# The decayed scores of a recurrence, one block size at a time: 64 strided query columns per size

## The chip, the cores and the metric

The kernel runs on one core of one Trainium2 chip. The metric is the device time of one execution in microseconds (us). A profile of one execution gives the busy time of each engine: TensorE (PE, with its weight loads as PEld), VectorE (DVE), ScalarE (ACT), GpSimd (POOL) and SyncE (SP, which issues the transfers).

## The reference, cut to what matters

One encoder layer over 16 meta tokens and 256 tokens, width 2048. Half of the mixing width is a recurrence with eight heads of width 128, whose keys decay by a forget gate per channel; the other half is a retention with four heads. A projection ahead of them, an output projection, two layer norms and a gated feed-forward block follow the usual way. What the change touches is the recurrence's scores:

```python
q = silu(q) * HG_HEAD_DIM ** -0.5
forget = lb + (1.0 - lb) * sigmoid(f_pre)
log_f, k = log(forget), 1.0 - forget
...
cum = cumsum(log_f)                     # over the tokens
decay = exp(where(causal, cum[t] - cum[s], -inf))      # per channel
scores = einsum('bhtk,bhsk,bhtsk->bhts', q, k, decay)
out = einsum('bhts,bhsv->bhtv', scores, v) + ...
```

So the score of query t and key s is the sum over 128 channels of q times k times the product of the forget gates from s + 1 to t. For t = s it is the plain product of q and k.

## The kernel before, in words

Weights come in blocks of 128 x 2048 fp32. ScalarE rounds a block to fp32r (`whi`, L75), VectorE takes the rest (`wlo`, L76), and each product of the projections is three matmuls (`whi` with the high part of the activations, `wlo` with it, `whi` with their low part). Three buffers hold each half, so a block's cast waits until TensorE has finished the block three before it. `project` (L317) uses one block for 128 output rows: 48 matmuls of 272 or 256 columns. `token_group` (L131) uses four blocks for a gate or the queries: 96 matmuls of 512 columns.

The recurrence and the retention are laid into this stream. `project` calls `tick` after every 12 matmuls, `token_group` after every 6; `steps` is a queue of pairs (ticks to wait, function), and a step issues its work when its ticks are over. The recurrence is done for a pair of heads at a time, `hgrn(pr, ...)`, four pairs: in pairs 0 and 2 a gate's `token_group` and then the retention's projections follow, in pairs 1 and 3 the retention's projections at once.

In `hgrn`, channels lie on partitions and tokens on the free axis: `Q` and `K` are 128 x 512 (two heads of 256 tokens; `K` has the meta tokens behind), `F` the forget gates. The scores `S` are 128 keys by 128 queries for each of four chunks. They are built by doubling: for block size b, a query in the second half of a block of 2b tokens meets the keys of its first half. `update(b)` then multiplies the queries of each second half by the decay of the first (`across(Q, ...)`), the keys of each first half by that of the second (`across(K, ...)`), and multiplies the block decays pairwise (`double`). Before, two sizes share one step: `E` holds three copied sets of 64 query columns per chunk, `scores` multiplies all of them with `K` in one product of 192 columns per chunk (L443, two PSUM banks of the name `sc`), and `merge` copies each set under a mask into `S` (L455). The diagonal is masked by the identity out of the first step's product (L488). `level32` (L517) and `level64` (L508) do the two largest sizes, `cross` (L528) the second 128 queries against the first 128 keys, `meta_scores` (L542) the meta tokens. `read_out` multiplies `S` with the values.

A scheduler sets the order on each engine from the order in which the code issues work; the engines run their own queues in order and wait for each other by semaphores.

Of the kernel before, what the change touches and what calls it, by code (L numbers as in the profile page):

```python
# [9 lines left out]
F32 = mybir.dt.float32  # L10
F32R = mybir.dt.float32r
I32 = mybir.dt.int32
# [26 lines left out]
def encoder_kernel(ctx: ExitStack, tc: tile.TileContext, x, meta, par, rows, w_in, w_out,  # L39
# [136 lines left out]
    make_identity(nc, ident)  # L176
    nhalf = cpool.tile([P, 8], F32, name="nhalf")
# [167 lines left out]
    with tc.tile_pool(name="att", bufs=1) as att:  # L345
        msk = att.tile([P, 7, 64], I32, name="msk")
# [35 lines left out]
        def hgrn(pr, qt, get_g):  # L382
# [29 lines left out]
            E = att.tile([P, 3, 4 * 64], F32, name="E")  # L412
# [24 lines left out]
            def scores():  # L437

                scs = []
                for o in (0, 2):  # L440
                    sc = pss.tile([P, 512], F32, name="sc")
                    for c in range(2):
                        nc.tensor.matmul(sc[:, c * 192:(c + 1) * 192], K[:, (o + c) * P:(o + c + 1) * P],  # L443
                                         E[:, :, (o + c) * 64:(o + c + 1) * 64], start=True, stop=True)
                    scs.append(sc[:, :384].rearrange("p (c m t) -> p c m t", c=2, m=3))
                return scs

            def targets(o, b):

                return [S[:, o:o + 2, :].rearrange("p c (n two b) -> p c n two b", two=2, b=b)[:, :, :, x, :]  # L450
                        for x in (1, 0)]

            def merge(scs, b, m, mask):
                for o, sc in zip((0, 2), scs):
                    nc.vector.copy_predicated(  # L455
                        out=targets(o, b)[0],
                        mask=msk[:, mask:mask + 1, :].broadcast_to([P, 2, 64]).rearrange("p c (n b) -> p c n b", b=b),
                        data=sc[:, :, m, :].rearrange("p c (n b) -> p c n b", b=b))

            def prepare(b):  # L460

                n = 2 * SEQ // (4 * b)
                nc.scalar.copy(E[:, 0, :].rearrange("p (n b) -> p n b", b=b), pairs(Q, b)[:, :, 1, :])
                across(Q, b, 2 * SEQ, True)
                far = pairs(Q, 2 * b)[:, :, 1, :]
                nc.scalar.copy(E[:, 1, :].rearrange("p (n b) -> p n b", b=2 * b), far)
                dv = state["d"][:, :2 * SEQ // b].rearrange("p (n four) -> p n four", four=4)
                nc.vector.tensor_tensor(out=E[:, 2, :].rearrange("p (n b) -> p n b", b=2 * b), in0=far,
                                        in1=dv[:, :, 1:2].broadcast_to([P, n, 2 * b]), op=ALU.mult)

            def first_queries():
                qv, fv = pairs(Q, 1), pairs(F, 1)
                state["d"] = F
                for x in range(2):
                    nc.scalar.copy(E[:, x, :], qv[:, :, x, 0])
                nc.vector.tensor_tensor(out=E[:, 2, :], in0=qv[:, :, 1, 0], in1=fv[:, :, 1, 0], op=ALU.mult)

            def levels_0_1():
                scs = scores()
                nc.vector.tensor_tensor(out=Q, in0=Q, in1=F[:, :2 * SEQ], op=ALU.mult)  # L480
                across(K, 1, W, False)
                across(Q, 1, 2 * SEQ, True)
                double(1)
                prepare(2)
                for o, sc in zip((0, 2), scs):
                    for x in range(2):
                        unit = ident.rearrange("p (n two) -> p n two", two=2)[:, :, x]
                        nc.vector.tensor_tensor(out=targets(o, 1)[1 - x][:, :, :, 0], in0=sc[:, :, x, :],  # L488
                                                in1=unit.unsqueeze(1).broadcast_to([P, 2, 64]), op=ALU.mult)
                merge(scs, 1, 2, 0)  # L490

            def levels(b, mask):
                scs = scores()
                across(K, b, W, False)
                double(b)
                across(Q, 2 * b, 2 * SEQ, True)
                across(K, 2 * b, W if 2 * b <= 8 else 2 * SEQ, False)
                double(2 * b)
                if b == 2:
                    prepare(8)  # L500
                merge(scs, b, 0, mask)
                merge(scs, 2 * b, 1, mask + 1)
                merge(scs, 2 * b, 2, mask + 2)

            def level64():
                sc = pss.tile([P, 512], F32, name="sc")
                for c in range(4):
                    nc.tensor.matmul(sc[:, c * 64:(c + 1) * 64], K[:, c * P:(c + 1) * P],  # L508
                                     Q[:, c * P + 64:(c + 1) * P], start=True, stop=True)
                update(64)  # L510
                nc.scalar.copy(S[:64, :, 64:], sc[:64, :256].rearrange("p (c t) -> p c t", c=4))
# [389 lines left out]
def _constants():  # L901
# [8 lines left out]
    for b in (2, 8):  # L910
        masks.append(level(b)[:, i // b % 2 == 1])
        for x in (1, 0):
            masks.append((level(2 * b) & (s // b % 2 == x))[:, i // (2 * b) % 2 == 1])
# [78 lines left out]
```

## Time and profile before

| | |
|---|---|
| median of 3 runs | 1293.54 us (1293.52 to 1295.84) |
| the profiled execution | 1293.27 us |
| its span, first to last instruction | 1291.5 us |
| busy: TensorE, VectorE, ScalarE, GpSimd | 98%, 58%, 42%, 1% of the span |
| mean granted TensorE clock | 0.997 of full speed |

The recurrence's steps lie between 62 and 432 us of the span. Times of rows are in us from the span's start. An fp32 product of the code is two matmul records in the trace.

### The profile page before, as it was taken

The page shows a single profiled execution, that of the slowest core. Times are in us where ns is not written, and L with a number is a line of the kernel's source. Part 1 is how long each engine was busy: PE and PEld are TensorE (multiplying, and loading weights), DVE is VectorE, ACT ScalarE, POOL GpSimd, SP SyncE. Part 2 cuts the span into 40 slices and gives each one's busy share as a digit, 9 for nine tenths or more (in the row PEclk, how much of TensorE's full clock was granted, in tenths as well). Part 3 has the DMA queues.
Part 4 walks back from the last instruction along what each step waited for, and adds up shares of the span by engine and source line. Part 5 has one row for each costly group of instructions (what it writes and reads, how often), then busy time and mean ns, then how long its engine had stood idle before and what let it go on. Part 6 is the DMA issues. An engine that isn't in the chain of part 4 may idle for free.

```text
span 1291.5 us, 17602 instructions
## 1 busy us (share of the span) xinstructions
PE 1266.2 (98%) x7516; PEld 1128.8 (87%) x7516; DVE 751.7 (58%) x872; ACT 547.1 (42%) x570; POOL 13.7 (1%) x27
## 2 busy tenths in 40 slices
PE   6999999999999999999999999999999999999996
PEld 4989999898999988878888888888888888888886
DVE  7765575565566585675555555444455555554565
ACT  7534334343343333574444444333344444444340
POOL 0000000000000000000000000000000000000000
PEclk9999999999999999999999999999999999999998
DMA  6644444444444377565555555455555555555551
GB/s 233 250 152 163 164 143 142 163 174 150 148 159 159 137 293 260 195 228 196 194 181 183 192 195 191 171 193 195 195 199 192 196 189 183 186 192 184 191 179 66
DMA packets 34958, 237.56 MB, mean 184 GB/s; under 512 B 4016, under 2 KB 4656, under 8 KB 6960
## 3 DMA queue, kind: packets, MB, share of 16 engines
q1 hardware_dynamic: 34880, 236.44, 52.1%
q8 instruction: 59, 0.97, 0.3%
q14 instruction: 19, 0.16, 0.0%
HBM read 234.33 MB, written 2.10 MB: 183 GB/s over the span
## 4 chain that ended last, share of the span: by engine, by line
PE 96%; DVE 1%; ACT 1%; DMA 0%; POOL 0%; issue 0%; SPq 0%; POOLq 0%; DVEq 0%
PE pp L131 34%; PE pp L841 23%; PE pp L317 22%; PE pp L846 12%; PE sc L443 1%; PE pp L123 1%; PE sc L623 1%; DMA xt<-in_x_dram 0%; ACT fl L225 0%; PE ms L555 0%; PE ms L552 0%; PE ms L375 0%; PE sc L542 0%; PE ms L636 0%; PE ms L635 0%; PE sc L508 0%
## 5 line engine op out<-in xcount | busy, mean ns | idle before, releaser
L76 DVE TENSOR_TENSOR wlo<-raw,whi 128x2048 fp32r<-128x2048 f32 (+1 forms) x211 | 479.0, 2271 | 391.9 <-ACT whi L75 390.2
L75 ACT CAST whi<-raw 128x2048 fp32r<-128x2048 f32 (+1 forms) x211 | 399.3, 1893 | 379.9 <-PE pp L131 202.7
L841 PE MATMUL pp<-h,whi 128*128 128x512 f32 x1280 | 305.4, 391 | 0.0
L841 PEld LDWEIGHTS pp<-h,whi 128*128 128x128 f32 x1280 | 235.3, 188 | 45.6
L317 PE MATMUL pp<-xhi,whi 128*128 128x272 f32 (+1 forms) x768 | 225.1, 293 | 0.0
L317 PE MATMUL pp<-xlo,whi 128*128 128x272 f32 (+1 forms) x768 | 219.9, 286 | 0.0
L317 PE MATMUL pp<-xhi,wlo 128*128 128x272 f32 (+1 forms) x768 | 219.1, 285 | 0.0
L131 PE MATMUL pp<-whi,t 128*128 128x512 f32 x648 | 199.8, 389 | 0.0
L846 PEld LDWEIGHTS pp<-h,wlo 128*128 128x128 f32 x1280 | 164.0, 191 | 6.2
L846 PE MATMUL pp<-h,wlo 128*128 128x256 f32 x1280 | 166.1, 283 | 0.0
L317 PEld LDWEIGHTS pp<-xhi,wlo 128*128 128x128 f32 x768 | 144.8, 189 | 0.4
L317 PEld LDWEIGHTS pp<-xhi,whi 128*128 128x128 f32 x768 | 144.7, 188 | 0.5
L317 PEld LDWEIGHTS pp<-xlo,whi 128*128 128x128 f32 x768 | 144.6, 188 | 0.0
L131 PEld LDWEIGHTS pp<-whi,t 128*128 128x128 f32 x648 | 121.6, 188 | 25.1
L131 PE MATMUL pp<-wlo,t 128*128 128x512 f32 x324 | 126.1, 389 | 0.0
L131 PEld LDWEIGHTS pp<-wlo,t 128*128 128x128 f32 x324 | 60.8, 188 | 12.6
L131 PE MATMUL pp<-whi,xhi 128*128 128x512 f32 x128 | 52.4, 412 | 1.8 <-ACT xhi L229 1.8
L131 PE MATMUL pp<-whi,xlo 128*128 128x512 f32 x128 | 51.2, 400 | 0.4 <-DVE xlo L230 0.4
L131 PE MATMUL pp<-wlo,xhi 128*128 128x512 f32 x128 | 51.5, 402 | 0.0
L131 PE MATMUL pp<-whi,mhi 128*128 128x512 f32 x120 | 46.9, 391 | 0.0
L131 PE MATMUL pp<-whi,mlo 128*128 128x512 f32 x120 | 46.7, 389 | 0.0
L131 PE MATMUL pp<-wlo,mhi 128*128 128x512 f32 x120 | 46.7, 389 | 0.0
(203 smaller groups left out, 963.8 us busy)
## 6 DMA issues: line engine op xcount, KB each, us to landing
raw<-in_w_gu_dram SPq DMA_DIRECT2D x88, 1024.0 KB, 4.9
raw<-in_w_in_dram SPq DMA_DIRECT2D x62, 1024.0 KB, 4.8
raw<-in_w_down_dram SPq DMA_DIRECT2D x44, 1024.0 KB, 4.9
raw<-in_w_out_dram SPq DMA_DIRECT2D x16, 1024.0 KB, 4.9
gb<-in_rows_dram SPq DMA_DIRECT2D x6, 1024.0 KB, 7.7
raw<-in_w_in_dram SPq DMA_DIRECT2D x4, 512.0 KB, 8.0
acc<-in_x_dram SPq DMA_DIRECT2D x2, 1024.0 KB, 6.0
out_dram<-acc SPq DMA_DIRECT2D x6, 256.0 KB, 2.4
```

The costliest lines, as they stand in the source:

```text
L75: nc.scalar.copy(hi[:, sl], raw[:, sl])
L76: nc.vector.tensor_tensor(out=lo[:, sl], in0=raw[:, sl], in1=hi[:, sl].bitcast(F32), op=ALU.subtract)
L123: nc.tensor.matmul(ph[:, :256], a, ws[k // 4][w][:, c:c + 256], start=(k == 0 and m == 0), stop=(k == 4 * n - 1 and m == 2))
L131: nc.tensor.matmul(ps[i], a, w[:, j * 512:(j + 1) * 512], start=(seen[i] == 0), stop=(left[i] == 0 and j == 3 and m == 2))
L317: nc.tensor.matmul(ps[:, :n], w[:, kc, :], a[:, kc, T - n:], start=(kc == 0 and j == 0), stop=(kc == KC - 1 and j == 2))
L443: nc.tensor.matmul(sc[:, c * 192:(c + 1) * 192], K[:, (o + c) * P:(o + c + 1) * P], E[:, :, (o + c) * 64:(o + c + 1) * 64], start=True, st ...
L623: nc.tensor.matmul(sc[:, c0:c0 + n], RK[:, k, k0:k0 + P], RQ[:, k, q0:q0 + n], start=(k == 0), stop=(k == 1))
L841: nc.tensor.matmul(ps, hi[:, kc, :], h[:, kc].rearrange("p m t -> p (m t)"), start=(kc == 0), stop=False)
L846: nc.tensor.matmul(ps[:, :SEQ], lo[:, kc, :], h[:, kc, 0, :], start=False, stop=(kc == KC - 1))
```

## The change

For each block size from 1 to 32 a step takes its 64 query columns per chunk straight out of `Q` with a stride, one product of 64 columns per chunk, and writes only one PSUM bank. The copies into `E` go. The diagonal comes from `own` = Q times K, multiplied with a column of ones (one column per chunk), and is spread by four activations over the identity. There are eight steps up to `level64` instead of six, and 29 ticks up to `meta_scores` instead of 25.

```diff
@@ -174,6 +174,8 @@
 
     ident = cpool.tile([P, P], F32, name="ident")
     make_identity(nc, ident)
+    ones = cpool.tile([P, 1], F32, name="ones")
+    nc.gpsimd.memset(ones, 1.0)
     nhalf = cpool.tile([P, 8], F32, name="nhalf")
     nc.gpsimd.memset(nhalf, -0.5)
 
@@ -343,7 +345,7 @@
     lnp_ctx.close()
 
     with tc.tile_pool(name="att", bufs=1) as att:
-        msk = att.tile([P, 7, 64], I32, name="msk")
+        msk = att.tile([P, 5, 64], I32, name="msk")
         nc.sync.dma_start(msk, masks)
         rp = att.tile([P, 2, T], F32, name="rp")
         nc.sync.dma_start(rp, rope)
@@ -409,7 +411,6 @@
 
 
 
-            E = att.tile([P, 3, 4 * 64], F32, name="E")
 
             def pairs(t, b, w=2 * SEQ):
                 return t[:, :w].rearrange("p (n two b) -> p n two b", two=2, b=b)
@@ -434,92 +435,47 @@
                 across(K, b, w, False)
                 double(b)
 
-            def scores():
-
-                scs = []
-                for o in (0, 2):
-                    sc = pss.tile([P, 512], F32, name="sc")
-                    for c in range(2):
-                        nc.tensor.matmul(sc[:, c * 192:(c + 1) * 192], K[:, (o + c) * P:(o + c + 1) * P],
-                                         E[:, :, (o + c) * 64:(o + c + 1) * 64], start=True, stop=True)
-                    scs.append(sc[:, :384].rearrange("p (c m t) -> p c m t", c=2, m=3))
-                return scs
-
-            def targets(o, b):
-
-                return [S[:, o:o + 2, :].rearrange("p c (n two b) -> p c n two b", two=2, b=b)[:, :, :, x, :]
-                        for x in (1, 0)]
-
-            def merge(scs, b, m, mask):
-                for o, sc in zip((0, 2), scs):
-                    nc.vector.copy_predicated(
-                        out=targets(o, b)[0],
-                        mask=msk[:, mask:mask + 1, :].broadcast_to([P, 2, 64]).rearrange("p c (n b) -> p c n b", b=b),
-                        data=sc[:, :, m, :].rearrange("p c (n b) -> p c n b", b=b))
-
-            def prepare(b):
-
-                n = 2 * SEQ // (4 * b)
-                nc.scalar.copy(E[:, 0, :].rearrange("p (n b) -> p n b", b=b), pairs(Q, b)[:, :, 1, :])
-                across(Q, b, 2 * SEQ, True)
-                far = pairs(Q, 2 * b)[:, :, 1, :]
-                nc.scalar.copy(E[:, 1, :].rearrange("p (n b) -> p n b", b=2 * b), far)
-                dv = state["d"][:, :2 * SEQ // b].rearrange("p (n four) -> p n four", four=4)
-                nc.vector.tensor_tensor(out=E[:, 2, :].rearrange("p (n b) -> p n b", b=2 * b), in0=far,
-                                        in1=dv[:, :, 1:2].broadcast_to([P, n, 2 * b]), op=ALU.mult)
-
-            def first_queries():
-                qv, fv = pairs(Q, 1), pairs(F, 1)
-                state["d"] = F
-                for x in range(2):
-                    nc.scalar.copy(E[:, x, :], qv[:, :, x, 0])
-                nc.vector.tensor_tensor(out=E[:, 2, :], in0=qv[:, :, 1, 0], in1=fv[:, :, 1, 0], op=ALU.mult)
-
-            def levels_0_1():
-                scs = scores()
-                nc.vector.tensor_tensor(out=Q, in0=Q, in1=F[:, :2 * SEQ], op=ALU.mult)
-                across(K, 1, W, False)
-                across(Q, 1, 2 * SEQ, True)
-                double(1)
-                prepare(2)
-                for o, sc in zip((0, 2), scs):
-                    for x in range(2):
-                        unit = ident.rearrange("p (n two) -> p n two", two=2)[:, :, x]
-                        nc.vector.tensor_tensor(out=targets(o, 1)[1 - x][:, :, :, 0], in0=sc[:, :, x, :],
-                                                in1=unit.unsqueeze(1).broadcast_to([P, 2, 64]), op=ALU.mult)
-                merge(scs, 1, 2, 0)
-
-            def levels(b, mask):
-                scs = scores()
-                across(K, b, W, False)
-                double(b)
-                across(Q, 2 * b, 2 * SEQ, True)
-                across(K, 2 * b, W if 2 * b <= 8 else 2 * SEQ, False)
-                double(2 * b)
-                if b == 2:
-                    prepare(8)
-                merge(scs, b, 0, mask)
-                merge(scs, 2 * b, 1, mask + 1)
-                merge(scs, 2 * b, 2, mask + 2)
-
-            def level64():
+            def odd_scores(b):
+
                 sc = pss.tile([P, 512], F32, name="sc")
                 for c in range(4):
                     nc.tensor.matmul(sc[:, c * 64:(c + 1) * 64], K[:, c * P:(c + 1) * P],
-                                     Q[:, c * P + 64:(c + 1) * P], start=True, stop=True)
-                update(64)
-                nc.scalar.copy(S[:64, :, 64:], sc[:64, :256].rearrange("p (c t) -> p c t", c=4))
+                                     pairs(Q, b)[:, c * 64 // b:(c + 1) * 64 // b, 1, :], start=True, stop=True)
+                return sc[:, :256].rearrange("p (c t) -> p c t", c=4)
+
+            def first():
+
+                own = att.tile([P, 2 * SEQ], F32, name="own", tag="sq")
+                nc.vector.tensor_tensor(out=own, in0=Q, in1=K[:, :2 * SEQ], op=ALU.mult)
+                dg = pss.tile([P, 512], F32, name="sc")
+                for c in range(4):
+                    nc.tensor.matmul(dg[:, c:c + 1], own[:, c * P:(c + 1) * P], ones, start=True, stop=True)
+                nc.vector.tensor_tensor(out=Q, in0=Q, in1=F[:, :2 * SEQ], op=ALU.mult)
+                state["d"] = F
+                od = att.tile([P, 4], F32, name="od")
+                nc.scalar.copy(od, dg[:, :4])
+                for c in range(4):
+                    nc.scalar.activation(S[:, c, :], ident, AF.Identity, scale=od[:, c:c + 1])
+
+            def level(b, mask):
+                sc = odd_scores(b)
+                update(b)
+                for o in (0, 2):
+                    nc.vector.copy_predicated(
+                        out=S[:, o:o + 2, :].rearrange("p c (n two b) -> p c n two b", two=2, b=b)[:, :, :, 1, :],
+                        mask=msk[:, mask:mask + 1, :].broadcast_to([P, 2, 64]).rearrange("p c (n b) -> p c n b", b=b),
+                        data=sc[:, o:o + 2, :].rearrange("p c (n b) -> p c n b", b=b))
 
             def level32():
-                sc = pss.tile([P, 512], F32, name="sc")
-                for c in range(4):
-                    for o in (0, 64):
-                        nc.tensor.matmul(sc[o:o + 32, c * 32:(c + 1) * 32], K[:, c * P + o:c * P + o + 32],
-                                         Q[:, c * P + o + 32:c * P + o + 64], start=True, stop=True)
+                sc = odd_scores(32)
                 update(32)
                 for o in (0, 64):
-                    nc.scalar.copy(S[o:o + 32, :, o + 32:o + 64],
-                                   sc[o:o + 32, :128].rearrange("p (c t) -> p c t", c=4))
+                    nc.scalar.copy(S[o:o + 32, :, o + 32:o + 64], sc[o:o + 32, :, o // 2:o // 2 + 32])
+
+            def level64():
+                sc = odd_scores(64)
+                update(64)
+                nc.scalar.copy(S[:64, :, 64:], sc[:64])
 
             def cross():
 
@@ -582,11 +538,10 @@
                     nc.vector.scalar_tensor_tensor(out=mlo[:, h, :], in0=ot[:, j * SEQ:(j + 1) * SEQ], scalar=g,
                                                    in1=mhi[:, h, :].bitcast(F32), op0=ALU.mult, op1=ALU.subtract)
 
-            steps.append((2, first_queries))
-            steps.append((2, levels_0_1))
-            steps.append((5, lambda: levels(2, 1)))
-            steps.append((5, lambda: levels(8, 4)))
-            steps.append((4, level32))
+            steps.append((4, first))
+            for n in range(5):
+                steps.append((3, lambda n=n: level(1 << n, n)))
+            steps.append((3, level32))
             steps.append((3, level64))
             steps.append((2, cross))
             steps.append((2, meta_scores))
...
-    masks = [level(1)[:, 1::2]]
-    for b in (2, 8):
-        masks.append(level(b)[:, i // b % 2 == 1])
-        for x in (1, 0):
-            masks.append((level(2 * b) & (s // b % 2 == x))[:, i // (2 * b) % 2 == 1])
+    masks = [level(b)[:, i // b % 2 == 1] for b in (1, 2, 4, 8, 16)]
```

On TensorE, the steps of the first pair between the value transposes (`ms<-ident,vt`) and `cross`. The projection matmuls between the rows are left out. Before:

```order
L443 MATMUL sc<-E,K 128x192 x4
...
L375 MATMUL ms<-ident,vt 128x128 x2
...
L443 MATMUL sc<-E,K 128x192 x4
...
L443 MATMUL sc<-E,K 128x192 x4
...
L517 MATMUL sc<-Q,K 32x32 x8
...
L508 MATMUL sc<-Q,K 128x64 x4
...
L528 MATMUL sc<-Q,K 128x128 x2
```

Now (the products of all sizes from 1 to 64 stand on one line, L442):

```order
L452 MATMUL sc<-ones,own 128x1 x4
...
L377 MATMUL ms<-ident,vt 128x128 x2
...
L442 MATMUL sc<-Q,K 128x64 x4
...
L377 MATMUL ms<-ident,vt 128x128 x2
...
L442 MATMUL sc<-Q,K 128x64 x4
...
L442 MATMUL sc<-Q,K 128x64 x4
...
L484 MATMUL sc<-Q,K 128x128 x2
```

The step of 192 columns has become one of one column at the same place; behind it stand seven steps of 64 columns (three are shown) where there were four of 192, 32 and 64, and 180 projection matmuls stand between the first step and `cross` instead of 138.

On VectorE, the end of the second pair's chain: the weight splits (`wlo`), the updates of `Q` and `K` by the block decays of sizes 32 and 64, and the scaling for `cross` (`D_2027` and `D_2089`). Before:

```order
L76 TENSOR_TENSOR wlo<-raw,whi 128x2048
L422 TENSOR_TENSOR Q<-Q,D_1880 128x8x32
L422 TENSOR_TENSOR K<-K,D_1880 128x8x32
L76 TENSOR_TENSOR wlo<-raw,whi 128x2048
L422 TENSOR_TENSOR Q<-Q,D_1965 128x4x64
L422 TENSOR_TENSOR K<-K,D_1965 128x4x64
```

Now:

```order
L423 TENSOR_TENSOR Q<-Q,D_1899 128x16x16
L423 TENSOR_TENSOR K<-K,D_1899 128x16x16
L464 COPY_PREDICATED S<-msk,sc 128x8x16 x2
L76 TENSOR_TENSOR wlo<-raw,whi 128x2048
L423 TENSOR_TENSOR Q<-Q,D_1964 128x8x32
L423 TENSOR_TENSOR K<-K,D_1964 128x8x32
L76 TENSOR_TENSOR wlo<-raw,whi 128x2048
L423 TENSOR_TENSOR Q<-Q,D_2026 128x4x64
L423 TENSOR_TENSOR K<-K,D_2026 128x4x64
```

A weight split still stands ahead of each of the last two updates; size 16 has its own update and its own two merges now, between splits as well.

## Rows read from the trace of the kernel before

**Rows 1.** The head of the page: the span, and each engine's busy time (share of the span) and instructions.
```profile
span 1291.5 us, 17602 instructions
PE 1266.2 (98%) x7516; PEld 1128.8 (87%) x7516; DVE 751.7 (58%) x872; ACT 547.1 (42%) x570; POOL 13.7 (1%) x27
```

**Rows 2.** The view by windows, for 38 to 456 us: length, busy time of the engines with their instructions, granted clock, share of DMA, GB/s.
```profile
38.00:456.00 418.00, 418.00 (x3100) 401.20 (x3099) 249.84 (x405) 167.70 (x203) 8.00 (x13) 1.00 0.46 161
```

**Rows 3.** The view of waits, TensorE's, of the whole run (the first and the only one behind 38 us): line that waited, line waited for, us in total, times, longest.
```profile
PE sc L235 <- DVE xt L216: 10.4, 1, 10.4
...
PE ms L235 <- ACT acc L748: 1.5, 1, 1.5
```

**Rows 4.** TensorE's timeline around the third `scores` of the first pair: start, length, instruction.
```profile
80.00 0.39 PE L131 MATMUL pp<-whi,xlo 128*128 128x512 f32 x1
80.22 1.46 PE L443 MATMUL sc<-E,K 128*128 128x192 f32 x8
...
81.75 0.40 PE L131 MATMUL pp<-wlo,xhi 128*128 128x512 f32 x1
```

**Rows 5.** The same around the first `scores`, in a stream of 272 columns.
```profile
62.45 0.29 PE L317 MATMUL pp<-xlo,whi 128*128 128x272 f32 x1
62.58 1.46 PE L443 MATMUL sc<-E,K 128*128 128x192 f32 x8
...
64.00 0.28 PE L317 MATMUL pp<-xhi,wlo 128*128 128x272 f32 x1
```

**Rows 6.** The same around `level32`.
```profile
86.85 0.40 PE L131 MATMUL pp<-whi,xlo 128*128 128x512 f32 x1
87.17 0.45 PE L517 MATMUL sc<-Q,K 128*32 128x32 f32 x16
...
87.89 0.40 PE L131 MATMUL pp<-wlo,xhi 128*128 128x512 f32 x1
```

**Rows 7.** The same around `level64`, `cross` and `meta_scores`.
```profile
91.59 0.40 PE L131 MATMUL pp<-whi,xlo 128*128 128x512 f32 x1
91.83 1.00 PE L508 MATMUL sc<-Q,K 128*128 128x64 f32 x8
...
92.96 0.40 PE L131 MATMUL pp<-wlo,xhi 128*128 128x512 f32 x1
...
95.28 0.40 PE L131 MATMUL pp<-whi,xlo 128*128 128x512 f32 x1
96.20 0.39 PE L131 MATMUL pp<-wlo,xhi 128*128 128x512 f32 x1
...
97.36 0.29 PE L317 MATMUL pp<-xhi,whi 128*128 128x272 f32 x1
...
98.74 0.29 PE L317 MATMUL pp<-xlo,whi 128*128 128x272 f32 x1
99.86 0.29 PE L317 MATMUL pp<-xhi,wlo 128*128 128x272 f32 x1
```

**Rows 8.** The same around the retention's scores, in a stream of 256 columns.
```profile
139.68 0.28 PE L317 MATMUL pp<-xhi,wlo 128*128 128x256 f32 x1
139.80 0.28 PE L317 MATMUL pp<-xlo,whi 128*128 128x256 f32 x1
139.91 1.87 PE L623 MATMUL sc<-RQ,RK 128*128 128x256 f32 x12
...
141.83 0.28 PE L317 MATMUL pp<-xhi,wlo 128*128 128x256 f32 x1
```

**Rows 9.** Groups of VectorE's and ScalarE's instructions between 38 and 456 us, by line and shape (the last one between 0 and 38 us): number, busy us and mean ns, idle time before them and what ended it.
```profile
L76 DVE TENSOR_TENSOR wlo<-raw,whi 128x2048 fp32r<-128x2048 f32 x63 | 144.2, 2291 | 88.1 <-ACT whi L75 87.9
L455 DVE COPY_PREDICATED S<-msk,sc 128x128 f32<-128x128 int32 x56 | 15.1, 346 | 0.1
L422 DVE TENSOR_TENSOR Q<-Q,D 128x256 f32<-128x256 f32 x24 | 10.1, 421 | 7.4 <-PE sc L508 6.9
L488 DVE TENSOR_TENSOR S<-sc,ident 128x128 f32<-128x128 f32 x16 | 3.9, 285 | 0.5
L468 DVE TENSOR_TENSOR E<-Q,D 128x256 f32<-128x256 f32 x8 | 3.6, 444 | 0.0
L480 DVE TENSOR_TENSOR Q<-Q,F 128x512 f32<-128x512 f32 x4 | 2.8, 689 | 0.0
L476 DVE TENSOR_TENSOR E<-Q,F 128x256 f32<-128x256 f32 x4 | 1.7, 422 | 0.0
...
L463 ACT COPY E<-Q 128x256 f32<-128x256 f32 x8 | 3.3, 416 | 2.0 <-PE sc L443 2.0
...
L225 ACT ACTIVATE fl<-ms,prm 128x128 f32<-128x128 f32 x15 | 5.8, 464 | 0.9 <-PE ms L235 0.9
```

**Rows 10.** The timeline of the second pair between `level64` and `cross`: ScalarE's cast, VectorE, TensorE; what ended an engine's idle time in brackets.
```profile
201.20 1.91 ACT L75 CAST whi<-raw 128x2048 fp32r<-128x2048 f32 x1
203.14 2.29 DVE L76 TENSOR_TENSOR wlo<-raw,whi 128x2048 fp32r<-128x2048 f32 x1 [3.93 <-ACT whi L75]
205.69 0.42 DVE L422 TENSOR_TENSOR K<-K,D 128x256 f32<-128x256 f32 x1
206.48 0.60 PE L528 MATMUL sc<-Q,K 128*128 128x128 f32 x4
```

**Rows 11.** The chain that ended last, one piece of it: start, us, number of matmuls.
```profile
817.51 130.59 PE pp L131 x576
```

## The prediction

> **What bounds the kernel now.** Read the head of the page first [rows 1]: a span of 1291.5 us, and TensorE busy in 98% of it, VectorE in 58%, ScalarE in 42%. Then the stretch in which the changed code runs, 38 to 456 us, by windows [rows 2]: TensorE is busy in 418.00 of 418.00 us, and its granted clock is 1.00 of full speed, the upper of its two levels (2.4 GHz). Then TensorE's waits [rows 3]: 10.4 us at its first transpose, and from 38 us on a single wait of 1.5 us, in layer norm 1 far behind the recurrence. So TensorE's sequence of products is the bound, and inside this stretch nothing makes it late. What VectorE and ScalarE save there is worth nothing by itself; what TensorE is given to do costs its full price, and a wait would be a new cost.
>
> **The price of a step, read from how far it pushes the stream.** Durations of single matmuls overlap, so I read the push: the distance from the last projection matmul ahead of a step to the second one behind it, less two ordinary distances. In the stream of 512-column matmuls the ordinary distance is 0.232 us (ten from 92.96 to 95.28), in that of 272 columns 0.126 (eleven from 97.36 to 98.74) [rows 7], of 256 columns 0.12 [rows 8]. An fp32 product stands in the trace as two records.
> - `scores`, four products of 192 columns, L443: 80.00 to 81.75 [rows 4] is 1.75, less 0.46 = 1.29 us; in the 272 stream 62.45 to 64.00 [rows 5] is 1.55, less 0.25 = 1.30. I take 1.30, that is 0.325 per product.
> - old `level32`, eight products of 32 by 32, L517: 86.85 to 87.89 [rows 6] is 1.04, less 0.46 = 0.58.
> - `level64`, four products of 64 columns, L508: 91.59 to 92.96 [rows 7] is 1.37, less 0.46 = 0.91; a product costs 0.225.
> - `cross`, two products of 128 columns, L528: 95.28 to 96.20 [rows 7] is 0.92, less 0.46 = 0.46, so 0.23 each. `meta_scores`, two of 256, L542: 98.74 to 99.86 [rows 7] is 1.12, less 0.25 = 0.87, so 0.43 each.
> - the retention's scores, L623: 139.80 to 141.83 [rows 8] is 2.03, less 0.24 = 1.79, for two products each of 256, 144 and 16 columns. The first two take 0.87 and, between 0.23 at 128 columns and 0.325 at 192, about 0.50; some 0.42 is left, 0.21 for a product of 16 columns.
>
> The list is flat below 128 columns: 16, 64 and 128 columns cost 0.21, 0.225 and 0.23. Only above that do columns count. A product pays for being a product.
>
> Here a rule of the Trainium skill speaks against that. "TensorE: Matmul & The Clock Gate", section "Back-to-back issue gap", gives an isolated warm matmul N / 2.4 + 2.5 ns; with four passes for an fp32 product, an estimate from that page, 64 columns would cost 0.117 us and 192 columns 0.33, and by the sum below the change would save 1.3 us per pair, some 1288 in all. The trace agrees at 192 columns (0.325) and not at 64 (0.225). The same page of the Trainium skill, section "LDWEIGHTS (loading the stationary operand)", gives columns / 1.2 ns for a load: two loads of 107 ns, 0.21 us, which fits the flat part and leaves the sum as it is below.
>
> **The change, part by part, for each of the four head pairs.**
> - Removed: three `scores` (3 x 1.30 = 3.90 us) and the eight small products (0.58): 4.48 us. `level64` stays as it is.
> - Added: four one-column products in `first`, five levels of four 64-column products, and `level32` now with four 64-column products: 28 products. For the 64 columns I take L508's 0.225, for the diagonal's one column the same (its bounds are 0.21, the 16-column remainder, and 0.23): 28 x 0.225 = 6.30 us.
> - Net: +1.82 us per pair, **+7.3 us** for four.
>
> Strided query columns: no row of before shows TensorE reading a moving operand with gaps. The 64 columns are spread over 128 positions, so if skipped positions were paid for, a level would cost as L528's 128 columns, 0.23 instead of 0.225: nothing more. From below I exclude a gain, since 16 columns in one piece already cost 0.21. Upper bound: each column taking four times as long, the price of 256 columns, 0.43: +0.83 us per level and pair, 3.3 us per level size. The Trainium skill, "SBUF — State Buffer", section "Door 1: The DMA port swizzle", says of SBUF's 16-byte lines that two hits in a line keep full bandwidth. Block sizes 1 and 2 have just two fp32 values in each line, larger ones four; by that the stride is free, which no run here shows yet. I take nothing.
>
> VectorE, per pair: 14 merges become 10, at 15.1 / 56 = 0.27 us each (-1.1); the four diagonal products (L488, -1.0), the two of L468 (-0.9) and L476 (-0.4) go; `own` comes, 512 columns as L480's (+0.69) [rows 9]. That is -2.7 us. ScalarE loses six copies into `E` (0.42 each by L463, -2.5) and gets four 128x128 activations and a 4-column copy (up to 0.46 each by L225, +2.3 at most) [rows 9]. Both are off the path [rows 2, 3], so I cost them at nothing. The memset of `ones` falls to GpSimd, busy 1% [rows 1]. The masks' transfer gets smaller. SyncE's order does not change.
>
> The new waits: from the first of the chain to `cross` TensorE had six steps per pair and has nine, so eight of them hang on the update before, 32 in all, where five per pair did. Between two levels lie 36 matmuls of 272 columns (4.53 us) or 18 of 512 (4.17). In that time VectorE must do two updates (0.42 each) and, by its order, usually one weight split of 2.29 [rows 9], which itself waits for ScalarE's cast: 3.1 us ahead of the next level, two merges behind it. That leaves about a microsecond. The tightest place is that of the second piece of order above, in the second pair: cast, split, then `update(64)`, then `cross`. In before the split starts at 203.14, the K update ends at 206.11 and `cross` starts at 206.48 [rows 10]: 0.37 us to spare. Afterwards the same three stand in the same order, with 25 matmuls of 256 columns between `level64` and `cross` (3.0 us) instead of 24 of 272 (3.0): 0.3 to 0.4 us to spare. I cost the waits at nothing; behind a late level all projections on TensorE would stand.
>
> **Sum.** The profiled execution took 1293.27 us (span 1291.5), which is 0.27 below the median of 1293.54. 1293.27 + 7.3 = **1300.6 us**, +0.55%. 0.2% of this kernel is 2.6 us, about what a measurement can tell from no change.
>
> **Rivals.**
> 1. Products are paid by their columns after all: 24 products of 64 columns would take 0.325 x 64 / 192 = 0.11 us each and the four of one column, say, half of that: 2.8 us, 1.7 below 4.48 per pair: 1286.6, faster. It decides when a 64-column product in a row of others costs less than 0.16 (4.48 / 28). L508 at 0.225 and the 16-column remainder speak against it. 4%. The first rule of the Trainium skill above points this way.
> 2. The strided reads are slow for sizes 1 and 2, at the 256-column price: +6.7, 1307. Nothing for it in the rows. 7%.
> 3. The updates come late: if nine of the 32 waits cost 0.7 us each, +6.3, 1307; the little to spare in the tight place is for it, against it that no such wait stands in [rows 3], though before had five such links per pair too. 8%.
> 4. No change within 0.2%, that is 1296.1 or less: the lighter VectorE and ScalarE let the projections run closer together, for instance the 288 matmuls of 512 columns in this stretch at 0.227 (as 576 of them do, 130.59 us [rows 11]) instead of 0.232: 1.4 us back; and the products at 0.21: 112 x 0.015 = 1.7 back. Both together give 1297.5; it decides only where a product costs 0.195 or less besides (112 x 0.03 = 3.4 back: 1295.8). 4%.
>
> The forecast has 77%, its own range 1299 to 1302.5. The range from 1298.5 to 1305 takes in the half-way cases of 2 and 3. Slower: 77 + 7 + 8 = 92%; same 4%; faster 4%.
>
> **What the changed profile would show.** Right: one line for all 64-column products (`level64` among them) with 224 matmul records, 28 steps that push the stream by 0.9 each, alike for all block sizes; the one-column step likewise 0.85 to 0.9; TensorE's table of waits still empty between 38 us and the output projection, that projection starting 7.3 us later, and everything behind it shifted by the same. Wrong: a push of 0.45 per step (rival 1), a larger push for block sizes 1 and 2 only (rival 2), or TensorE waiting for VectorE's Q or K (rival 3).

## The result, and the profile after

The changed kernel takes 1301.03 us, the median of 4 executions (1300.12 to 1301.62), beside 1293.80 for the kernel before on the same chip (1293.52 to 1295.84): a ratio of 1.0052, 95% interval 1.0040 to 1.0064. It is slower, by 7.2 us where 7.3 were forecast. (On one chip two executions, one of the kernel before and one of e7_narrow_twice, took about twice as long as the others, 2573 and 2575 us; they are left out, and e7b is that same kernel measured on another chip.)

The profiled execution took 1301.62 us. The head of its page answers to [rows 1]:

```profile
span 1299.6 us, 17699 instructions
PE 1274.2 (98%) x7580; PEld 1137.4 (88%) x7580; DVE 744.9 (57%) x832; ACT 542.9 (42%) x566; POOL 13.8 (1%) x28
```

The view by windows from 38 us to the output projection answers to [rows 2]: TensorE is busy throughout, at the upper level of its clock.

```profile
38.00:463.00 425.00, 425.00 (x3164) 409.30 (x3163) 241.74 (x362) 162.97 (x199) 7.30 (x12) 1.00 0.45 160
```

The view of waits, TensorE's from 38 us to the end, has the one line of [rows 3] and no other:

```profile
PE ms L237 <- ACT acc L703: 1.5, 1, 1.5
```

TensorE's groups in that stretch, by line and shape, with number, busy us and mean ns: all 64-column products are on one line, and the one-column products beside them take about as long.

```profile
L442 PE MATMUL sc<-Q,K 128*128 128x64 f32 x224 | 28.0, 267 | 0.0
...
L452 PE MATMUL sc<-ones,own 128*128 128x1 f32 x32 | 3.8, 239 | 0.0
```

TensorE's timeline around the one-column step (62.23 to 63.37) and around block size 1 (67.98 to 69.12), which answers to [rows 5]:

```profile
62.23 0.29 PE L319 MATMUL pp<-xlo,whi 128*128 128x272 f32 x1
62.35 0.95 PE L452 MATMUL sc<-ones,own 128*128 128x1 f32 x8
63.16 0.37 PE L319 MATMUL pp<-xhi,whi 128*128 128x272 f32 x1
63.37 0.29 PE L319 MATMUL pp<-xhi,wlo 128*128 128x272 f32 x1
...
67.98 0.29 PE L319 MATMUL pp<-xlo,whi 128*128 128x272 f32 x1
68.11 1.00 PE L442 MATMUL sc<-Q,K 128*128 128x64 f32 x8
68.92 0.37 PE L319 MATMUL pp<-xhi,whi 128*128 128x272 f32 x1
69.12 0.28 PE L319 MATMUL pp<-xhi,wlo 128*128 128x272 f32 x1
```

Both are 1.14 long, less two ordinary distances (0.25): a push of 0.89. Read in the same way, the steps of 64 columns (28: seven block sizes, `level64` among them, in four pairs) push by 0.88 to 0.90, whatever the block size, and the four of one column by 0.89. Two of the 28, size 64 in pairs two and four, stand right behind transpositions and can't be read from the matmul ahead; from their own first record to the second matmul behind them it is 1.01, as around block size 1 (68.11 to 69.12).

**One distance that holds the whole change.** From the first query transposition (L392 before, L394 after) to the first matmul of the output projection, TensorE does all the steps and nothing else differs in its work. Before (the first two rows) that is 409.40 us, after (the last two) 416.46:

```profile
47.02 0.60 PE L392 MATMUL ms<-ident,qt 128*128 128x128 f32 x4
...
456.42 0.40 PE L131 MATMUL pp<-whi,mhi 128*128 128x512 f32 x1
```

```profile
46.78 0.60 PE L394 MATMUL ms<-ident,qt 128*128 128x128 f32 x4
...
463.24 0.40 PE L131 MATMUL pp<-whi,mhi 128*128 128x512 f32 x1
```

So the steps cost 7.06 us more. By the pushes it is 28 x 0.89 = 24.92 for what was added (per pair the one-column step and sizes 1 to 32), less 4 x 4.48 = 17.92 for what went: 7.0. I call this distance the stretch below. One trace was kept of each kernel, so how well the stretch repeats was not measured as such. A distance that no kernel here changes tells: from the output projection's first matmul to TensorE's last one it is 823.9 to 824.0 us in the kernel before and in all nine experiments of the table, where whole times of one kernel scatter by 1 to 4 us.

**The rest of the span's 8.1.** The output projection starts 6.82 later than before (this execution reached the stretch 0.24 earlier), but the end is 8.1 later. The other 1.25 us (TensorE takes 825.2 from there to its end, not 824.0) are lost in one place. After TensorE's wait in layer norm 1, which both kernels have (1.5 us), the matmuls of 512 columns stand 0.43 apart instead of 0.23:

```profile
559.98 0.66 PE L237 MATMUL ms<-ident,acc 128*128 128x128 f32 x4 [1.47 <-ACT acc L703]
...
562.52 1.05 PE L131 MATMUL pp<-whi,h 128*128 128x512 f32 x2
563.37 0.63 PE L131 MATMUL pp<-wlo,h 128*128 128x512 f32 x1
```

The view by windows has a granted clock of 0.85 there:

```profile
562.00:572.00 10.00, 10.00 (x42) 8.11 (x41) 7.21 (x12) 9.58 (x22) 0.00 (x0) 0.85 0.67 233
```

In the kernel before, the same work stands at 1.00:

```profile
555.00:565.00 10.00, 10.00 (x47) 7.94 (x45) 7.59 (x13) 10.00 (x23) 0.00 (x0) 1.00 0.72 230
```

The clock fell to its lower level (1.2 instead of 2.4 GHz) for some 3 us in this execution: 3 of the 10 us at half clock make 0.85. None of the experiments on the changed kernel shows it behind the same wait, so nothing ties it to the change.

### The profile page after: what moved, and what is told of

Same layout as the page of the kernel before. It is cut to its first block, busy times and chain, and to the rows that moved or that the text cites. A ratio compares the mean times of both kernels' runs of the same rounds, so it can differ in the third digit from the quotient of the medians.

```text
span 1299.6 us, 17699 instructions
## 1 busy us (share of the span) xinstructions
PE 1274.2 (98%) x7580; PEld 1137.4 (88%) x7580; DVE 744.9 (57%) x832; ACT 542.9 (42%) x566; POOL 13.8 (1%) x28
## 4 chain that ended last, share of the span: by engine, by line
PE 96%; DVE 2%; DMA 0%; ACT 0%; POOL 0%; issue 0%; SPq 0%; POOLq 0%; DVEq 0%
PE pp L131 33%; PE pp L796 22%; PE pp L319 22%; PE pp L801 12%; PE sc L442 2%; PE pp L123 1%; PE sc L578 1%; DMA prm<-in_par_dram 0%; DVE wlo L76 0%; PE ms L511 0%; PE ms L508 0%; PE ms L377 0%; PE ms L590 0%; PE ms L591 0%; PE sc L498 0%; PE sc L452 0%
```

## The experiments

Each ratio is taken against executions of the kernel before on the experiment's own chip; the stretch comes from the one trace of each kernel, and "against" says how it differs from another's. The code cuts are shortened, and some of their lines say in words what the code does.

| kernel | median us | ratio to before (95%) | stretch us | against |
|---|---|---|---|---|
| before | 1293.80 | 1 | 409.40 | |
| changed | 1301.03 | 1.0052 (1.0040 to 1.0064) | 416.46 | before +7.06 |
| e1_wide | 1300.98 | 1.0058 (1.0044 to 1.0071) | 416.44 | changed -0.02 |
| e3_nodiag | 1297.88 | 1.0036 (1.0023 to 1.0049) | 412.78 | changed -3.68 |
| e2_old32 | 1299.32 | 1.0036 (1.0024 to 1.0049) | 415.25 | changed -1.21 |
| e5_narrow64 | 1293.61 | 1.0000 (0.9991 to 1.0008) | 409.04 | before -0.36 |
| e7b | 1295.93 | 1.0014 (1.0004 to 1.0024) | 410.89 | e5_narrow64 +1.85 |
| e4_tick2 | 1300.59 | 1.0055 (1.0041 to 1.0069) | 416.34 | changed -0.12 |
| e10_tick1 | 1302.82 | 1.0066 (1.0053 to 1.0079) | 419.05 | changed +2.59 |
| e8_pack | 1288.60 | 0.9957 (0.9945 to 0.9969) | 404.41 | before -4.99 |
| e9_pack4 | 1286.16 | 0.9937 (0.9924 to 0.9951) | 402.04 | before -7.36 |

**Does the stride cost, do columns count?** (e1_wide, sizes 1 to 16)

```diff
-  pairs(Q, b)[:, c * 64 // b:(c + 1) * 64 // b, 1, :]   # 64 strided columns
+  Q[:, c * P:(c + 1) * P]                               # all 128, in one piece; merge picks the odd blocks
```

> The changed kernel, but each level from 1 to 16 multiplies a chunk's keys with all 128 of its queries in one piece (no stride, twice the columns), and the merge picks the odd ones. Theory (a product costs two loads of its 128 stationary columns as long as its columns take less): the push of a level goes from 0.89 to 0.91 us, the price of cross per product, so +0.4 us over the changed kernel, about 1301.4. Rival (columns are paid): twice the columns, up to +0.89 per level, 20 levels, +18 us. Rival (the stride costs something that the contiguous columns save): a push below 0.89.

```profile
L464 PE MATMUL sc<-Q,K 128*128 128x128 f32 x160 | 21.0, 274 | 0.0
L442 PE MATMUL sc<-Q,K 128*128 128x64 f32 x64 | 8.0, 268 | 0.0
```

The pushes are 0.89 to 0.90 with twice the columns and no gaps, as with 64 strided ones, and the stretch is the same (not even the 0.4 us that I expected came). Stride and columns both cost nothing here.

**What does the one-column step cost?** (e3_nodiag)

```diff
-  own = Q * K;  four products dg = own x ones;  od = copy of dg
-  nc.scalar.activation(S[:, c, :], ident, AF.Identity, scale=od[:, c:c + 1])
+  nc.scalar.activation(S[:, c, :], ident, AF.Identity, scale=ones)
```

> The changed kernel without the diagonal's own product: no Q times K and no one-column products; the identity is scaled by ones instead, so the diagonal of the scores is left out (it becomes 1). Theory (a one-column product costs as much as one of 64 columns): 0.89 us per pair less, -3.6 us against the changed kernel, about 1297.4. Rival (columns are paid): one column next to nothing, so no change, 1301.

The stretch is 3.68 shorter, 0.92 per pair (its push was 0.89; 3.6 in all was expected), and a product of one column costs what one of 128 does. The 0.03 per pair beyond the push is not explained.

**The largest size put back.** (e2_old32: `level32` with its eight 32 by 32 products of before)

> The changed kernel with the largest block size but one put back: level32 does its eight 32 by 32 products as in the kernel before; all other sizes keep their 64 strided columns. My theory (a product has a flat price per product, set by its 128 stationary columns rather than by its moving ones): the step's push falls from 0.89 to the 0.58 us that it had in the kernel before, 0.31 us per pair, 1.25 us in all: 299.8 above 1000, that is about 1299.8, ratio to the kernel before 1.0046. Rival (a price per product whatever its shape, 0.22 us): eight products cost 1.76 us, +0.87 per pair, +3.5 us: about 1304.5.

```profile
94.53 0.40 PE L131 MATMUL pp<-whi,xlo 128*128 128x512 f32 x1
94.85 0.45 PE L473 MATMUL sc<-Q,K 128*32 128x32 f32 x16
...
95.57 0.39 PE L131 MATMUL pp<-wlo,xhi 128*128 128x512 f32 x1
```

The step pushes by 0.58 again (1.04 less 0.46), 0.31 less per pair; the stretch is 1.21 shorter. Eight small products are cheaper than four of 128 by 64: the price isn't one per product either.

**What does the flat price follow?** The stationary operand (the keys, which are loaded ahead of a matmul) was left to vary. e5_narrow64 is the kernel before with `level64` over only the 64 keys whose scores are copied into `S`; e7b does each of these products twice.

```diff
-  nc.tensor.matmul(sc[:, c * 64:(c + 1) * 64], K[:, c * P:(c + 1) * P], ...)
+  nc.tensor.matmul(sc[:64, c * 64:(c + 1) * 64], K[:, c * P:c * P + 64], ...)
```

> The kernel before, with level64's four products over the 64 keys that are used instead of 128 (64 stationary columns, 64 moving). Theory (the floor below 128 moving columns is the load of the stationary columns, twice per fp32 product): both loads are halved, the push of level64 falls from 0.91 to about 0.5 us, -1.6 us for four pairs, about 1292. Rival (a fixed price per product whatever its size): the push stays at 0.91, no change.

> The kernel before with level64 over its 64 stationary keys and each of its four products done twice, the same kernel as in the run whose execution stood at about half speed throughout. Only the push of this step is asked for: once over 64 keys it was 0.83 us. Theory A (a product over 64 stationary columns costs about 0.15 us, and the change of the tile's shape some 0.2 us per step): 0.83 + 4 x 0.15 = 1.43 us. Theory B (a narrow product costs as much as a wide one): 0.83 + 4 x 0.215 = 1.7 us.

TensorE's timeline around this step in e7b (16 records), then the same place in e5_narrow64 (8):

```profile
92.29 0.40 PE L131 MATMUL pp<-whi,xlo 128*128 128x512 f32 x1
92.62 1.15 PE L509 MATMUL sc<-Q,K 128*64 128x64 f32 x16
93.69 0.51 PE L131 MATMUL pp<-whi,xhi 128*128 128x512 f32 x1
94.04 0.40 PE L131 MATMUL pp<-wlo,xhi 128*128 128x512 f32 x1
```

```profile
92.31 0.40 PE L131 MATMUL pp<-whi,xlo 128*128 128x512 f32 x1
92.65 0.68 PE L508 MATMUL sc<-Q,K 128*64 128x64 f32 x8
93.25 0.51 PE L131 MATMUL pp<-whi,xhi 128*128 128x512 f32 x1
93.60 0.40 PE L131 MATMUL pp<-wlo,xhi 128*128 128x512 f32 x1
```

The distances are 1.75 and 1.29 us, less 0.46: pushes of 1.29 and 0.83. So the 0.83 of e5_narrow64 met neither of its two expectations, 0.5 and 0.91. Four more narrow products cost 0.46, 0.115 each (the stretch says the same: 1.85 / 16 = 0.116), half of the 0.22 to 0.225 with 128 stationary columns. Theory B (1.7) is out; theory A (1.43) had the direction and too high a price. Nor are e7b's products cheap because each meets the same keys twice in a row: inside the step the records start 0.058 apart in e7b and in e5_narrow64 alike. So the flat price goes with the stationary columns.

What keeps e5_narrow64 from gaining is a fixed cost beside the products: 0.83 - 4 x 0.115 = 0.37 us per step. With 128 stationary columns throughout there is none to see: two products push by 0.45 (`cross`), four by 0.89. The weight loads show where it arises; the first row is of the kernel before, the others of e5_narrow64:

```profile
91.59 1.10 PEld L508 LDWEIGHTS sc<-Q,K 128*128 128x128 f32 x8
```

```profile
92.64 0.54 PEld L508 LDWEIGHTS sc<-Q,K 128*64 128x64 f32 x8 [0.37 <-issue]
93.25 0.19 PEld L131 LDWEIGHTS pp<-whi,xhi 128*128 128x128 f32 x1
```

Before, the first load starts 0.24 us ahead of its matmul (91.83 in [rows 7]), together with the projection matmul ahead. With the narrow tile the first load starts only with its matmul (92.65), and so does the first wide load behind the step (93.25). The old `level32`, with 32 stationary columns, has the same: its 16 records start within 0.25 us (87.17 to 87.42 in the kernel before), so some 0.3 us of its push of 0.58 are not the products'. Changing the tile's shape for four products eats most of what the halved price gives. The Trainium skill, "TensorE: Matmul & The Clock Gate", section "LDWEIGHTS (loading the stationary operand)", gives columns / 1.2 ns per load, an estimate of 0.107 us for two loads of 64 columns and 0.213 for two of 128; the runs agree (0.115 and 0.22).

**How much room have the updates?** The prediction gave a link about a microsecond to spare. e4_tick2 and e10_tick1 take the ticks between two levels from three to two and to one, and put them ahead of `cross`.

```diff
-  steps.append((3, lambda n=n: level(1 << n, n)))     # level32, level64 likewise; cross 2
+  steps.append((2, lambda n=n: level(1 << n, n)))     # e4_tick2;  cross 9
+  steps.append((1, lambda n=n: level(1 << n, n)))     # e10_tick1; cross 16
```

> The changed kernel with levels, size 32 and size 64 only two ticks apart (24 matmuls of 272 columns, 3.0 us, or 12 of 512, 2.8 us) instead of three, and seven ticks more ahead of cross, so that all behind stays in place. Theory (three ticks hide the update chain with about a microsecond to spare): where a split of 2.29 us stands between two levels, the 3.1 us of work plus two merges no longer fit, TensorE waits for Q or K about 0.3 to 1 us at some of the links: +3 to +10 us, and the view of waits names VectorE's Q or K. Rival (the chain has far more room than reckoned): no wait, no change, 1301.

> The changed kernel with the links of the chain as tight as the queue lets them be: from the second block size on one tick between two levels instead of three (12 matmuls of 272 columns, 1.5 us, or 6 of 512, 1.4 us), and the ticks that are saved put ahead of the product across the chunks, so that everything behind that stands where it stood. Between two levels VectorE needs the two updates, about 0.8 us with what lies around them, and where a weight split of 2.3 us comes first, 3.1 us. Theory A (my margin in the prediction: a split may stand between any level and the next update): at two links or so per pair TensorE waits about 1 us or more, eight links, +5 to +10 us over the changed kernel, 1306 to 1311. Theory B (the splits lie where VectorE waits for TensorE anyway, so that only the updates count): 0.8 us fits into 1.5, no waits, 1300 to 1301.5 as the changed kernel.

With two ticks all pushes stay at 0.88 to 0.90; my expectation fell. With one, 10 of the 28 steps push by 1.08 to 1.17, the others that can be read in this way by 0.89 to 0.95: the stretch grows by 2.59, so theory A's five to ten microseconds fall too, and so does theory B's zero. The table of waits is empty even here: a matmul record of this stream is 0.29 long and the next one starts 0.13 behind its start, so a wait of 0.2 leaves hardly a gap between records. The timeline shows it, TensorE and then VectorE in e10_tick1:

```profile
69.50 1.00 PE L442 MATMUL sc<-Q,K 128*128 128x64 f32 x8
...
71.15 0.29 PE L319 MATMUL pp<-xhi,whi 128*128 128x272 f32 x1
71.47 1.08 PE L442 MATMUL sc<-Q,K 128*128 128x64 f32 x8
72.35 0.37 PE L319 MATMUL pp<-xhi,wlo 128*128 128x272 f32 x1
...
70.54 0.43 DVE L423 TENSOR_TENSOR Q<-Q,D 128x256 f32<-128x256 f32 x1 [1.07 <-PE sc L442]
70.88 0.44 DVE L423 TENSOR_TENSOR K<-K,D 128x272 f32<-128x272 f32 x1
```

The product ends at 70.50, Q's update runs from 70.54 to 70.97, K's to 71.32, and the next product starts at 71.47 instead of 71.28. So a late product follows the end of `K`'s update by 0.15 us, and 1.97 from start to start of two levels is all that a link needs when no weight split falls into it; here only 7 matmuls (0.9 us) and the first level's own push lie between. In the changed kernel two levels start 5.05 to 5.75 us apart, so over 3 us are to spare instead of one. Where a split does fall in between it takes a part of that: the shortest distance from the end of `K`'s update to the next level's product is 1.82 us (pairs two and four), still far from 0.15. Where the split mostly went, VectorE's timeline of the changed kernel shows:

```profile
80.41 0.49 DVE L464 COPY_PREDICATED S<-msk,sc 128x128 f32<-128x128 int32 x2
80.81 2.28 DVE L76 TENSOR_TENSOR wlo<-raw,whi 128x2048 fp32r<-128x2048 f32 x1
84.79 0.42 DVE L423 TENSOR_TENSOR Q<-Q,D 128x256 f32<-128x256 f32 x1 [1.69 <-PE sc L442]
```

Here it stands behind one level's merges, and VectorE still waits 1.69 us for the next level's product before it may update, so that split delays nothing.

**A version that beats both.** If products cost the same up to 128 columns, two sets of 64 belong in one product. e8_pack, built on the kernel before, gets the set without its own block's decay by dividing it out, so that it fits the same `K` as the next size; e9_pack4 does the same for sizes 32 and 64. The division is by products of up to 8 forget gates in e8_pack and 32 in e9_pack4; the runs show nothing of inputs that bring such a product near zero.

```diff
-  E: three sets; 4 products of 192 columns; steps (diagonal, 1), (2, 4), (8, 16), 32, 64
+  r = reciprocal(decay of the odd blocks)
+  E[0] = Q (odd blocks of b) * r;  then update Q and K by b;  E[1] = Q (odd blocks of 2b)
+  4 products of 128 columns;  e9_pack4: (diagonal, 1), (2, 4), (8, 16), (32, 64)
```

> The kernel before with two sets of 64 query columns per product instead of three: the set that mattered was the smaller block size's with and without its decay; here the queries without it are had by dividing (VectorE's reciprocals of the block decay), so that sizes 1 and the diagonal, 2 and 4, 8 and 16 each share one product of 128 columns. The three steps that pushed by 1.30 us each should push by the price of four 128-column products, 4 x 0.22 to 0.23 = 0.89 to 0.92. My theory (flat price up to 128 columns): 12 steps x 0.39 = 4.7 us less than before, about 1288.5, ratio 0.9964. Rival (128 columns cost two thirds of 192, 0.217, so the same) can't be told apart here; rival 2 (the longer work on VectorE ahead of the first step and of the others makes TensorE wait): waits of TensorE for VectorE between 62 and 432 us, and less or nothing won: 1290 to 1295.

> The kernel that packs two sets of 64 query columns into each product, with the sizes 32 and 64 packed the same way: one step of four 128-column products in place of the steps of 0.58 (eight 32 by 32 products) and 0.91 us. My theory: this step pushes by 0.89 to 0.90; per pair 0.58 less, 2.3 us less in all than with the separate steps (0.9957 of the kernel before), 4 x (5.39 - 3.57) = 7.3 us less than the kernel before: ratio 0.9943, 1286.5 or so. Rival (the longer chain on VectorE, with one more reciprocal and multiplication ahead of the last of these steps, makes TensorE wait, or the step across the chunks behind it): a push over 0.95 at that step or at the next one, and part of the 2.3 us lost.

TensorE's groups in e9_pack4 (L478 is the step of the diagonal and size 1):

```profile
L441 PE MATMUL sc<-E,K 128*128 128x128 f32 x96 | 12.7, 275 | 0.0
L478 PE MATMUL sc<-Q,KD 128*128 128x128 f32 x32 | 4.2, 274 | 0.0
```

The packed steps push by 0.89 and `cross`, behind them, by 0.44 to 0.45, as ever; no wait stands in the stretch. It is 4.99 shorter (expected 4.7) and 7.36 (expected 7.3); e9_pack4 takes 0.63% less time than the kernel before and, by the two ratios, 1.1% less than the changed one (0.9937 / 1.0052 = 0.9886). The rival's late chain on VectorE, whose busy time in e9_pack4 is 758.9 us against 751.7 [rows 1], did not come.

## Why the prediction was right, point by point

- **The bound.** Right: TensorE is busy in 425.00 of 425.00 us, the table has no wait there, and VectorE's and ScalarE's savings (6.8 and 4.2 us of busy time by the heads of the pages) bought nothing. The 10.8 us that VectorE was to save (4 x 2.7) was too high, which costs nothing off the path.
- **Added.** 28 products x 0.225 = 6.30 per pair; measured 7 steps x 0.89 = 6.23. The one-column product was put at the price of 64 columns, and it has it (0.89 a step).
- **Removed.** 4.48 per pair, from [rows 4 to 6]; what it leaves by the stretch, (7.06 - 24.92) / 4 = -4.47, is the same.
- **"A product pays for being a product".** Wrong as a reason, and the number did not need it. The prediction's own row of `level32`, eight products for 0.58 us (0.07 each), spoke against it; e2_old32 and e7b show that the price goes with the stationary columns, 0.22 us for 128 and 0.115 for 64. The sum came out because each of the 28 added products has 128 of them and so has L508, from which the price was read.
- **Stride at nothing.** Right: sizes 1 and 2 push as the others, and contiguous columns change nothing. The remark of the Trainium skill that was drawn on, "SBUF — State Buffer", "Door 1: The DMA port swizzle", is in accord with it. Rival 2 is out.
- **Rival 1** is out: 64 columns cost 0.22, not 0.11. The N / 2.4 + 2.5 ns of the Trainium skill ("TensorE: Matmul & The Clock Gate", section "Back-to-back issue gap") is the gap of an isolated matmul, as the section says itself; here, where the stationary operand changes with each product, it doesn't give the price at 64 columns.
- **Rival 4** is out: projections don't run closer together. The ordinary distances are 0.23 and 0.126 as before, and the products cost 0.22.
- **Waits at nothing.** Right in the sum, wrong in the working. "That leaves about a microsecond" counted a split of 2.3 us between a level and its update, where the split mostly stands in VectorE's own idle time; 1.8 us or more lie between the end of `K`'s update and the next level's product, mostly 2.8 to 3.9. And the tight place, "0.3 to 0.4 us to spare", had none. The 0.37 of before counted the 0.15 that even a late product needs behind the update as spare. In the second pair now the split again waits for its cast, `K`'s update ends at 215.76, and `cross` starts 0.16 behind it:

```profile
212.79 2.29 DVE L76 TENSOR_TENSOR wlo<-raw,whi 128x2048 fp32r<-128x2048 f32 x1 [4.30 <-ACT whi L75]
...
215.34 0.42 DVE L423 TENSOR_TENSOR K<-K,D 128x256 f32<-128x256 f32 x1
215.92 0.67 PE L484 MATMUL sc<-Q,K 128*128 128x128 f32 x4
```

  It pushes by 0.50 instead of 0.45 in pairs two and four, and by 0.44 to 0.45 in all four pairs of e4_tick2, which gives it nine ticks and whose stretch is 0.12 shorter. So the update is barely late there, by 0.1 us in all (rival 3 had 6.3); the table shows no wait. That the waits came to next to nothing is luck in part: the links had more room than was reckoned, the tight place less.
- **The sign "everything behind shifted by 7.3"** failed in this execution: 6.8 at the output projection, 8.1 at the end. The clock's fall between the two is not in the sum. Whether the other executions behind the median (+7.2) had it, the record doesn't show.

## What to carry to other kernels

Where TensorE is the bound, price a small product by the push that it gives to the stream around it, not by its columns or its recorded length: here four fp32 products over 128 stationary columns cost 0.89 us with 1, 64 or 128 moving columns, so what counts is how often a stationary block is presented. Splitting a product that is filled past the flat part into several that are not (192 columns into three of 64) makes it dearer; filling products exactly to the flat part's end made the fastest kernel. A fixed pair of points in the program, with only the change between them, told 0.1 us where whole times scatter by one us and more.

## What the runs showed of the hardware that was not expected

- A change of tile shape in the stream (128 to 64 stationary columns and back) costs 0.3 to 0.4 us per step, nearly as much as the halved price gave back over four products (0.83 against 0.91 us); over eight it would have paid, 1.29 against eight times 0.22.
- TensorE's granted clock fell to the lower level behind a wait of 1.47 us in one profiled execution (1.25 us lost) and not in the others behind the same wait. What decides it, the runs don't show.
- A wait of about 0.2 us ahead of a matmul does not appear in the table of waits; it shows only in the distance from one start to the next.
